# A two-layer streaming encoder step: the head's squares on GpSimd wait for the first weight tile's low part, which is made in halves, and the first feed-forward's down-weight sums get later turns

## The chip, the cores and the metric

One core of one Trainium2 chip. The metric is the device time of the whole kernel in microseconds (us), the median of the timed runs. Before the change it is 2237.28 us, the median of three runs between 2237.07 and 2242.95 us.

## The reference

One inference step of two layers on 1024 prompt frames and 64 sample frames of width 1024. Layer 0 mixes tokens by sliding-window attention with 16 query heads and 4 key heads, layer 1 by a diagonal state-space model. Each mixer and each feed-forward stands between two norms:

```python
for i in range(DEPTH):
    hp = rms_norm(xp, g_pre_mix[i])
    mp = attn_prompt(hp, ...) if i % 2 == 0 else s5_mixer(hp, ...)
    xp = xp + rms_norm(mp, g_post_mix[i])
    hp = rms_norm(xp, g_pre_ffn[i])
    fp = conv_ffn(hp, prev, w_up[i], conv_w[i], conv_b[i], w_down[i])
    xp = xp + rms_norm(fp, g_post_ffn[i])
```

`rms_norm` divides by the root of the mean square over the 1024 channels and multiplies by a gain. `conv_ffn` projects up to 5632 channels, applies a causal convolution of width 3, multiplies the gelu of one half by the other half, and projects down. All is float32.

## The kernel before, in words

The 1088 frames are three blocks of 384, 384 and 320 columns; channels lie on the 128 partitions, eight tiles of them (k = 0 to 7) make the width. A float32 product is made of three matmuls (`mm3`, L224 to L226): with the operand and the weight each split into a high part, rounded to the fast matmul type, and a low part, the rest. L224 multiplies the weight's high part by the operand's low part `hl`, L225 high by high part `hh`, L226 the weight's low part by `hh`. So the third matmul of each k needs the weight's low part.

**Weights** come in units of 128 x 1024 through `raw` (two buffers) by DMAs that SyncE (SP) issues. `split_unit` (L217) makes the high part on ScalarE (ACT) and the low part on VectorE (DVE), both into a tile `whl` of a pool of six. Loads run two units ahead of use (`unit`, `load_ahead`).

**The head** (`build`, from L1532) loads the input and calls `pre_norm` for the three blocks. For each k, ACT makes `hh` (L301) and DVE makes `hl` (L307); for the blocks after the first, GpSimd (POOL) makes three of the eight `hl`, through `gx` (L304, L305). `rstd` sums the squares: for the first block POOL squares two k at a time (L253, four instructions), for the others ACT does (L255); DVE adds (L257, L261). TensorE (PE) then sums over the partitions (L267), DVE finds the root (L272 to L292), PE spreads it over the partitions (L285), and ACT copies it to `rb` (L309). Until the first weight is ready PE runs 14 matmuls on an identity (`fill`, L231). TensorE's first real work is three products of the first block: a key tile (unit 1), and two query tiles (units 2 and 3).

**The first feed-forward** (`ffn` with i = 0) takes 44 up-projection units. Per unit it has 72 matmuls in three blocks; DVE multiplies the results by `rb` into `u` (L415, L417), `conv` (L423 to L425) and `gate` follow, and SP stores the gated tile to `gd` (L442, L443). Beside this, in steps called turns (`aside`, one per unit, 44 in all), run two more jobs:

- *sums*: the down-projection is done with seven products in place of eight, for which sums of the weights (`sums_w`) and of the gated tiles (`sums_g`) are made on DVE. One job is: SP loads `jt` (L356 or L368), in the next turn four additions (L359 to L362, L371 to L377), then SP stores (L363, L378). The dictionary `starts` says in which turn each begins: `sums_w(k)` for k = 0 to 10 in turns 1, 3, ... 21, `sums_g(k)` in turns 24, 26, ... 44.
- *preparation of the state-space layer* (`ssm_prep`), in eight rounds q = 0 to 7: DVE makes `ct` (L1042 to L1047) and `w` (L890 to L895), PE multiplies (`kps`, L1070, and `wps`, L1084), DVE copies to `kt` (L1074, L1075), SP stores it as `kd` and reads it back in another layout with eight DMAs (`tl`, L1105), ACT rearranges (`tp`), and SP stores `prm` from `oc`, `tp` and `b` (L1051, L1107, L1086).

**What sets the order.** Nothing of this is placed by hand on an engine. A scheduler replays the program on a modelled clock and gives each engine, among the instructions that are ready in its model, the one with the smallest priority number; the number counts up as the code emits instructions, and `later(1500)` adds 1500 for the preparation. Each engine, and SP's queue of DMAs, then works strictly in the order found. `order(x, first)` forces an order between two instructions in the schedule; a dependency of class `NoSync` adds no semaphore, one of class `Sync` does.

Of the kernel before, what the change touches and what calls it, by code (L numbers as in the profile page):

```python
# [8 lines left out]
F32 = mybir.dt.float32  # L9
F32R = mybir.dt.float32r  # L10
I32 = mybir.dt.int32
AF = mybir.ActivationFunctionType
# [4 lines left out]
D = 1024  # L17
# [17 lines left out]
KH = KF // 2  # L35
# [8 lines left out]
class Core:  # L44
# [65 lines left out]
    def big(self, shape, name, dt=F32R):  # L110
        return self.wts.tile(shape, dt, name=name, tag="big", bufs=6)

    def order(self, x, first):

        dep = mybir.DependencyInfo(mybir.DependencyClass.NoSync, mybir.DependencyReason.DATA)
        self.tc.add_manual_dep(x.ins, first.ins.name, dep, reason="order")

    @contextmanager
# [13 lines left out]
    sq = {}  # L132
# [77 lines left out]
        return self.split_unit(raw)  # L210

    behind = ()

    def split_unit(self, raw):
        nc = self.nc
        w = self.big([P, 2, D], "whl")
        x = nc.scalar.activation(w[:, 0], raw, AF.Copy), nc.vector.tensor_sub(w[:, 1], raw, w[:, 0].bitcast(F32))  # L217
        for u, v in zip(x, self.behind):
            self.order(u, v)
        return w  # L220
# [17 lines left out]
    def rstd(self, src, n, tag, root, bcast=True, first=False, alt=None, adder=None, fine=False):  # L238
        nc = self.nc
        adder = adder or nc.vector  # L240
        acc = None
        for q in range(4):
            sq = self.n2(n, tag)
            xq = src[:, 2 * q:2 * q + 2]
            if fine and q == 3:

                adder.tensor_add(acc[:, 0], acc[:, 0], acc[:, 1])
                for j in range(2):
                    nc.scalar.activation(sq[:, j], xq[:, j], AF.Square)
                    adder.tensor_add(acc[:, 0], acc[:, 0], sq[:, j])  # L250
                break
            if first:
                nc.gpsimd.tensor_mul(sq, xq, xq)  # L253
            else:
                self.sq[q] = nc.scalar.activation(sq, xq, AF.Square)  # L255
            if q:
                adder.tensor_add(acc, acc, sq)  # L257
            else:
                acc = sq
        else:  # L260
            adder.tensor_add(acc[:, 0], acc[:, 0], acc[:, 1])  # L261
        cuts = [min(c, n - P) for c in range(0, n, P)]
        nt = len(cuts)
        pr = self.sm_ps("pr", int(tag == "sqb") if alt is None else alt)
        st = pr[:, 384:384 + nt]
        for i, c in enumerate(cuts):
            self.last_st = nc.tensor.matmul(st[:, i:i + 1], acc[:, 0, c:c + P], self.ones, start=True, stop=True)  # L267
        v = self.small.tile([P, 4, 4], F32, name="nv" + tag, bufs=3)
        x, hx, r, t = (v[:, i, :nt] for i in range(4))
        if root:  # L270
            nc.scalar.activation(x, st, AF.Sqrt, bias=self.eps)
            nc.vector.tensor_scalar(hx, st, 1e-6, -0.5, op0=ALU.add, op1=ALU.mult)  # L272
            nc.vector.reciprocal(r, x)
            self.refine(r, t, hx)
        else:

            nc.vector.tensor_scalar(x, st, 1e-6, None, op0=ALU.add)
            ri = r.bitcast(I32)
            nc.vector.tensor_scalar(ri, x.bitcast(I32), 1, None, op0=ALU.logical_shift_right)
            nc.vector.tensor_scalar(hx, x, -0.5, None, op0=ALU.mult)  # L280
            nc.vector.tensor_scalar(ri, ri, -1.0, float(MAGIC), op0=ALU.mult, op1=ALU.add)
            for _ in range(3):
                self.refine(r, t, hx)
        for i, c in enumerate(cuts if bcast else []):
            self.last_tr = nc.tensor.transpose(pr[:, c:c + P], r[:, i:i + 1].to_broadcast([P, P]), self.ident)  # L285
        return pr, r
# [54 lines left out]
    def ffn(self, i, h, rb, after, side=None, beside=lambda: None, x=None, g=None):  # L341

        nc, tc, a = self.nc, self.tc, self.a
# [10 lines left out]
        def sums_w(k):  # L354
            x = (jt[:, :2048] if i == 0 else self.yp.tile([P, 2048], F32, name="jw", tag="ypB", bufs=1)).rearrange("p (c h m) -> p c h m", c=2, h=2)
            Q.dma_start(x, a["w_down"][i, k::KH].rearrange("c p (h m) -> p c h m", h=2))  # L356
            yield
            a11, a12, a21, a22 = x[:, 0, 0], x[:, 1, 0], x[:, 0, 1], x[:, 1, 1]
            E.tensor_add(a22, a21, a22)  # L359
            E.tensor_sub(a21, a11, a21)  # L360
            E.tensor_sub(a11, a22, a11)
            E.tensor_sub(a12, a12, a11)  # L362
            Q.dma_start(sd[:, k], x)  # L363

        def sums_g(k):
            x = jt[:, k % 2 * 1536:k % 2 * 1536 + 1536] if i == 0 else ts.tile([P, 1536], F32, name="jg", tag="t2")
            x = x.rearrange("p (c b t) -> p c b t", c=2, b=2)
            Q.dma_start(x, gd[:, k::KH, :768].rearrange("p c (b t) -> p c b t", b=2))  # L368
            yield
            a11, a12, a21, a22 = x[:, 0, 0], x[:, 0, 1], x[:, 1, 0], x[:, 1, 1]  # L370
            v = E.tensor_sub(a11, a12, a11)  # L371
            if i == 1:

                self.order(v, self.last_conv)
            E.tensor_sub(a12, a22, a12)
            E.tensor_sub(a22, a22, a11)
            E.tensor_sub(a21, a21, a22)  # L377
            Q.dma_start(td[:, k], x)  # L378


        w0 = (PLAIN + 1) * i
        starts = {2 * (k + w0) + 1: sums_w(k) for k in range(KH)}
        starts.update({2 * (k + KH) + 2: sums_g(k) for k in range(KH)})
        jobs = {}

# [1223 lines left out]
```

## Time and profile before

| what | us |
|---|---|
| timed runs: median (lowest, highest) | 2237.28 (2237.07, 2242.95) |
| the profiled execution's own time | 2241.03 |
| its span | 2239.2 |
| TensorE busy | 2191.6 (98%) |
| VectorE busy | 1661.3 (74%) |
| ScalarE busy | 1042.3 (47%) |
| GpSimd busy | 412.8 (18%) |

All times in the traces count from the start of the span. TensorE is the busy engine, so time is gained or lost where it stands still: the difference of span and busy time is 47.6 us for the whole kernel. A wait is listed with the engine and line that it was put down to. In the timeline each row has the start, the length, the engine, the line, the operation, what is written and read, and the count; in brackets the idle time before it. Rows of several like instructions are merged. SPq is SP's queue, which issues DMAs; the length is that of the issue, not of the transfer.

### The profile page before, as it was taken

Reading aid. Unit: us, or ns where it says so; the run is one execution under the profiler, and the core shown is the slowest. Engines: PE = TensorE matmul, PEld = TensorE weight load, DVE = VectorE, ACT = ScalarE, POOL = GpSimd, SP = SyncE. Lnnn points to the kernel's source line nnn. Section 1 sums busy time; section 2 is a strip of 40 time slices with the busy share of each in tenths; the row PEclk is TensorE's granted clock in tenths of the full one; section 3 lists DMA queues with packets and bytes.
Section 4 is the critical chain, followed back from the end, with each engine's and each line's share of the span. In section 5 each row is a group of like instructions: output and inputs, shape, how many; then the busy total and the mean of one; then the engine's idle time right before and its main releaser. Section 6 shows DMA issues by size and latency. Waiting matters only on the chain.

```text
span 2239.2 us, 35982 instructions
## 1 busy us (share of the span) xinstructions
PE 2191.6 (98%) x13875; PEld 2117.1 (95%) x13875; DVE 1661.3 (74%) x2886; ACT 1042.3 (47%) x1890; POOL 412.8 (18%) x474
## 2 busy tenths in 40 slices
PE   9999999999999999999988899999999999999997
PEld 8987789999999999999986699999999999999997
DVE  8687647989878877767758855597976776676764
ACT  5255747422343342555545641263555455455543
POOL 5322004200032423000200034352010110110000
PEclk9999999999999999999999899999999999999999
DMA  5100015655355565887749888752266686579772
GB/s 197 37 22 29 20 62 158 241 188 202 122 150 173 176 208 187 274 279 236 233 163 339 263 280 294 249 167 75 87 224 229 218 297 226 196 272 314 218 253 97
DMA packets 208123, 428.47 MB, mean 191 GB/s; under 512 B 23312, under 2 KB 114224, under 8 KB 205008
## 3 DMA queue, kind: packets, MB, share of 16 engines
q1 hardware_dynamic: 175648, 326.56, 44.2%
q0 software_dynamic: 23984, 95.12, 11.9%
q10 hardware_dynamic: 8320, 4.49, 0.8%
q8 instruction: 109, 1.79, 0.3%
q14 instruction: 62, 0.51, 0.1%
HBM read 297.75 MB, written 128.37 MB: 190 GB/s over the span
## 4 chain that ended last, share of the span: by engine, by line
PE 32%; DMA 13%; DVE 9%; issue 4%; ACT 2%; POOL 2%; SPq 0%; DVEq 0%; ACTq 0%; POOLq 0%
PE mm L224 10%; PE mm L226 10%; PE mm L225 10%; DMA sj<-in_w_up 3%; DMA raw<-in_w_down 2%; DMA jw<-in_w_down 2%; DMA raw<-sd 1%; POOL sj L1391 1%; DMA yd<-ys 1%; DVE whl L217 1%; DMA su<-sj 1%; DMA gd<-t 1%; DVE gt L564 1%; DVE t L425 1%; DMA yf<-yd 1%
## 5 line engine op out<-in xcount | busy, mean ns | idle before, releaser
L224 PE MATMUL mm<-hl,whl 128*128 128x384 f32 (+1 forms) x1960 | 643.3, 329 | 4.1 <-DVE hl L307 3.1
L226 PE MATMUL mm<-hh,whl 128*128 128x384 f32 (+1 forms) x1960 | 641.2, 329 | 2.3 <-DVE whl L217 2.3
L225 PE MATMUL mm<-hh,whl 128*128 128x384 f32 (+1 forms) x1960 | 643.1, 328 | 0.0
L224 PEld LDWEIGHTS mm<-hl,whl 128*128 128x128 f32 x1960 | 368.4, 188 | 6.5 <-DVE hl L307 4.7
L226 PEld LDWEIGHTS mm<-hh,whl 128*128 128x128 f32 x1960 | 368.4, 188 | 3.0 <-DVE whl L217 2.9
L225 PEld LDWEIGHTS mm<-hh,whl 128*128 128x128 f32 x1960 | 368.6, 188 | 0.1
L217 DVE TENSOR_TENSOR whl<-raw,whl 128x1024 fp32r<-128x1024 f32 x202 | 254.9, 1263 | 146.7 <-ACT whl L217 146.2
L217 ACT ACTIVATE whl<-raw 128x1024 fp32r<-128x1024 f32 x202 | 213.0, 1058 | 248.1 <-PE mm L226 128.6
L224 PE MATMUL mm<-gt,whl 128*128 128x384 f32 (+1 forms) x968 | 316.8, 327 | 2.9 <-ACT whl L217 2.4
L226 PE MATMUL mm<-gt,whl 128*128 128x384 f32 (+1 forms) x968 | 315.8, 327 | 0.7 <-DVE whl L217 0.7
L225 PE MATMUL mm<-gt,whl 128*128 128x384 f32 (+1 forms) x968 | 315.9, 327 | 0.0
L224 PEld LDWEIGHTS mm<-gt,whl 128*128 128x128 f32 x968 | 181.7, 188 | 3.7 <-ACT whl L217 2.6
L226 PEld LDWEIGHTS mm<-gt,whl 128*128 128x128 f32 x968 | 181.7, 188 | 1.2 <-DVE whl L217 1.2
L225 PEld LDWEIGHTS mm<-gt,whl 128*128 128x128 f32 x968 | 181.8, 188 | 0.0
L195 DVE TENSOR_TENSOR whl<-raw,whl 128x1024 fp32r<-128x1024 f32 x84 | 96.4, 1154 | 72.7 <-ACT whl L194 71.3
L424 DVE SCALAR_TENSOR_TENSOR t<-u,ppt,t 128x1090 f32<-128x1090 f32 x88 | 126.9, 1443 | 5.8 <-ACT t L423 4.1
L194 ACT ACTIVATE whl<-raw 128x1024 fp32r<-128x1024 f32 x84 | 82.6, 987 | 101.8 <-DMA raw<-sd 40.1
L423 ACT ACTIVATE t<-u,ppt 128x1090 f32<-128x1090 f32 x88 | 114.2, 1298 | 26.2 <-DVE u L520 13.6
L425 DVE SCALAR_TENSOR_TENSOR t<-u,ppt,t 128x1090 f32<-128x1090 f32 x88 | 122.0, 1386 | 0.4
L415 DVE TENSOR_TENSOR u<-rb,mm 128x384 f32<-128x384 f32 (+1 forms) x164 | 80.8, 504 | 31.2 <-PE mm L226 26.4
L438 ACT ACTIVATE t<-t 128x1090 f32<-128x1090 f32 x44 | 49.1, 1115 | 113.1 <-DVE t L425 113.1
L564 DVE TENSOR_TENSOR gt<-gr,gt 128x768 fp32r<-128x768 f32 (+2 forms) x106 | 90.5, 881 | 11.1 <-ACT gt L563 10.2
(389 smaller groups left out, 4141.5 us busy)
## 6 DMA issues: line engine op xcount, KB each, us to landing
raw<-in_w_up SPq DMA_DIRECT2D x88, 512.0 KB, 4.4
raw<-in_w_down SPq DMA_DIRECT2D x74, 512.0 KB, 4.4
raw<-sd SPq DMA_DIRECT2D x40, 512.0 KB, 4.9
sj<-in_w_up POOLq DMA_DIRECT2D x68, 256.0 KB, 6.1
su<-sj POOLq DMA_DIRECT2D x34, 512.0 KB, 5.9
raw<-su SPq DMA_DIRECT2D x34, 512.0 KB, 4.6
pm<-prm SPq DMA_DIRECT2D x32, 522.0 KB, 8.2
gr<-td SPq DMA_DIRECT2D x40, 384.0 KB, 5.6
```

Of the source, the lines that this page charges most:

```text
L194: nc.scalar.activation(w[:, 0], raw, AF.Copy)
L195: nc.vector.tensor_sub(w[:, 1], raw, w[:, 0].bitcast(F32))
L217: x = nc.scalar.activation(w[:, 0], raw, AF.Copy), nc.vector.tensor_sub(w[:, 1], raw, w[:, 0].bitcast(F32))
L224: nc.tensor.matmul(out, w[:, 0, sl], xl, start=start, stop=False, skip_group_check=more)
L225: nc.tensor.matmul(out, w[:, 0, sl], xh, start=False, stop=False, skip_group_check=more)
L226: self.last_mm = nc.tensor.matmul(out, w[:, 1, sl], xh, start=False, stop=stop, skip_group_check=more)
L415: nc.vector.tensor_mul(u[:, t0 + 2:t0 + 2 + np_], rb[:, t0:t0 + np_], ps[:, :np_])
L423: nc.scalar.activation(t, u[:, 0:T + 2], AF.Identity, bias=cb(m), scale=cw(0, m))
L424: nc.vector.scalar_tensor_tensor(t, u[:, 1:T + 3], cw(1, m), t, op0=ALU.mult, op1=ALU.add)
L425: self.last_conv = nc.vector.scalar_tensor_tensor(t, u[:, 2:T + 4], cw(2, m), t, op0=ALU.mult, op1=ALU.add)
L438: nc.scalar.activation(ta, ta, AF.Gelu_apprx_tanh)
L564: nc.vector.tensor_sub(x[:, 1, u], raw, x[:, 0, u].bitcast(F32))
```

## The change

Three edits. The first unit's `split_unit` makes its high and its low part in two halves of 512 columns (k 0 to 3, then k 4 to 7). In `rstd` of the first block, POOL's first square gets a true wait (class `Sync`) for the second half of that low part. In the first feed-forward `sums_w(k)` begins in turn min(2k + 5, 12 + k) in place of 2k + 1: turns 5, 7, ... 17, 19, 20, 21, 22.

```diff
-    def order(self, x, first):
+    def order(self, x, first, kind=mybir.DependencyClass.NoSync):
-        dep = mybir.DependencyInfo(mybir.DependencyClass.NoSync, mybir.DependencyReason.DATA)
+        dep = mybir.DependencyInfo(kind, mybir.DependencyReason.DATA)
...
+    first_lo = None
     def split_unit(self, raw):
         nc = self.nc
         w = self.big([P, 2, D], "whl")
+        if self.first_lo is None:
+            for c in (slice(0, 512), slice(512, D)):
+                nc.scalar.activation(w[:, 0, c], raw[:, c], AF.Copy)
+                self.first_lo = nc.vector.tensor_sub(w[:, 1, c], raw[:, c], w[:, 0, c].bitcast(F32))
+            return w
...
             if first:
-                nc.gpsimd.tensor_mul(sq, xq, xq)
+                x = nc.gpsimd.tensor_mul(sq, xq, xq)
+                if q == 0:
+                    self.order(x, self.first_lo, mybir.DependencyClass.Sync)
...
-        starts = {2 * (k + w0) + 1: sums_w(k) for k in range(KH)}
+        starts = {2 * (k + w0) + 1 if i else min(2 * k + 5, 12 + k): sums_w(k) for k in range(KH)}
```

Below, lines of the changed kernel are 7 to 9 higher than the same lines before (L307 is L316, L257 is L266, L217 is L224). What stands on DVE at the very start, from the first low part of the operand on, before:

```order
L307 SCALAR_TENSOR_TENSOR hl<-y,ppt,hh 128x384 x2
L217 TENSOR_TENSOR whl<-raw,whl 128x1024
L307 SCALAR_TENSOR_TENSOR hl<-y,ppt,hh 128x384 x3
L257 TENSOR_TENSOR sqb<-sqb 128x768
L307 SCALAR_TENSOR_TENSOR hl<-y,ppt,hh 128x384 x3
L217 TENSOR_TENSOR whl<-raw,whl 128x1024
L257 TENSOR_TENSOR sqb<-sqb 128x768
```

And on the same engine at the same place in the changed kernel:

```order
L316 SCALAR_TENSOR_TENSOR hl<-y,ppt,hh 128x384 x2
L222 TENSOR_TENSOR whl<-raw,whl 128x512 x2
L316 SCALAR_TENSOR_TENSOR hl<-y,ppt,hh 128x384 x6
L266 TENSOR_TENSOR sqb<-sqb 128x768
L224 TENSOR_TENSOR whl<-raw,whl 128x1024
```

The first addition of squares has moved behind all eight low parts of the first block, and the second addition behind the second unit's low part and the first rows of the next block.

The other place is SP's queue late in the first feed-forward, from the eight reads of round q = 6 of the preparation on. Before (`gd` is the gated tile, `jt` the tile of a sums job, `prm` the prepared parameters):

```order
L1105 DMA tl<-kd 16x8x128 x8
L192 DMA raw<-in_w_down 128x2x512
L442 DMA gd_3999<-t 128x1024
L443 DMA gd_3999<-t 128x64
L1107 DMA prm<-tp 128x4x256
L368 DMA jt<-gd_3999 128x2x768
L1086 DMA prm<-b_6908 128x4x256
L192 DMA raw<-in_w_down 128x2x512
```

The same stretch of SP's queue in the changed kernel:

```order
L1114 DMA tl<-kd 16x8x128 x8
L192 DMA raw<-in_w_down 128x2x512
L1116 DMA prm<-tp 128x4x256
L451 DMA gd_4001<-t 128x1024
L452 DMA gd_4001<-t 128x64
L1095 DMA prm<-b_6899 128x4x256
L377 DMA jt<-gd_4001 128x2x768
L192 DMA raw<-in_w_down 128x2x512
```

The store of the prepared `tp` has moved ahead of the store of the gated tile, and the load of `jt`, which reads `gd` back, behind the store of `b`. The same exchange stands in rounds 2 and 4. On PE the `kps` products of rounds 2 to 6 stand 11 matmuls of the main product further forward, those of rounds 1 and 7 five; those of round 0 stand 11 further back. Up to the last store of a `sums_w` job, SP's queue has the same order in both kernels, so the loads and stores of these jobs have not moved in it.

## The prediction

> **What bounds the kernel now.** I read the page's busy times first, then TensorE's list of waits, then the timeline of the head, and last the stretch of the first feed-forward in which instructions move. The page gives the scale:
>
> ```profile
> span 2239.2 us, 35982 instructions
> PE 2191.6 (98%) x13875; PEld 2117.1 (95%) x13875; DVE 1661.3 (74%) x2886; ACT 1042.3 (47%) x1890; POOL 412.8 (18%) x474
> ```
>
> TensorE stands still for 2239.2 - 2191.6 = 47.6 us in all, so no edit that only removes waits can bring more than that, and a measurement of this kernel can tell about 0.3%, 6.7 us, from no change. TensorE's list of waits shows how little of it lies where the change works (us in total, times, longest):
>
> ```profile
> PE p L1258 <- DMA pm<-prm: 4.6, 5, 2.2
> PE mm L224 <- DVE hl L307: 3.1, 3, 1.6
> PE mm L226 <- DVE whl L217: 3.0, 3, 1.9
> ```
>
> The third row is the head: the longest, 1.9 us, is TensorE waiting for the first weight's low part. The timeline of the head shows why it is late:
>
> ```profile
> 5.36 1.47 POOL L253 TENSOR_TENSOR sqb<-y 128x768 f32<-128x768 f32 x1 [4.29 <-DMA y<-in_x]
> 5.37 1.12 ACT L301 ACTIVATE hh<-y,ppt 128x384 fp32r<-128x384 f32 x2 [3.15 <-DMA y<-in_x]
> 6.02 1.75 DVE L307 SCALAR_TENSOR_TENSOR hl<-y,ppt,hh 128x384 fp32r<-128x384 f32 x2 [4.70 <-ACT hh L301]
> 6.56 1.06 ACT L217 ACTIVATE whl<-raw 128x1024 fp32r<-128x1024 f32 x1
> 7.62 1.47 POOL L253 TENSOR_TENSOR sqb<-y 128x768 f32<-128x768 f32 x1 [0.80 <-DMA y<-in_x]
> 7.69 2.48 DVE L217 TENSOR_TENSOR whl<-raw,whl 128x1024 fp32r<-128x1024 f32 x1
> 10.10 1.66 DVE L307 SCALAR_TENSOR_TENSOR hl<-y,ppt,hh 128x384 fp32r<-128x384 f32 x3
> 10.23 0.69 PE L226 MATMUL mm<-hh,whl 128*128 128x384 f32 x1 [1.94 <-DVE whl L217]
> ...
> 12.55 3.21 DVE L307 SCALAR_TENSOR_TENSOR hl<-y,ppt,hh 128x384 fp32r<-128x384 f32 x3
> 12.71 1.78 POOL L253 TENSOR_TENSOR sqb<-y 128x768 f32<-128x768 f32 x1 [3.62 <-DVE sqb L257]
> 14.47 1.54 POOL L304 TENSOR_SCALAR gx<-y,ppt 128x384 f32<-128x384 f32 x1
> 14.95 0.19 PEld L224 LDWEIGHTS mm<-hl,whl 128*128 128x128 f32 x1 [0.22 <-DVE hl L307]
> 15.68 1.21 DVE L217 TENSOR_TENSOR whl<-raw,whl 128x1024 fp32r<-128x1024 f32 x1
> 15.81 0.19 PEld L224 LDWEIGHTS mm<-hl,whl 128*128 128x128 f32 x1 [0.39 <-DVE hl L307]
> 16.95 0.45 PE L226 MATMUL mm<-hh,whl 128*128 128x384 f32 x1 [0.34 <-DVE whl L217]
> ```
>
> The same subtraction takes 2.48 us beside a square on POOL and 1.21 us without one; three `hl` take 1.66 us alone and 3.21 us beside a square. So a square holds VectorE up by 1.2 to 1.5 us wherever it meets it.
>
> **The head, step by step.** Without the squares `hl` 0 and 1 end at about 7.15 (ACT ends the second `hh` at about 6.5, and one `hl` takes 1.66 / 3 = 0.55). A half of the low part is 1.21 / 2 = 0.6, with its own overhead 0.7; its first high half comes from ACT at about 7.25. So the halves end at about 8.0 and 8.7, and not at 10.17: 1.5 us earlier, and TensorE's third matmul starts at about 8.1 in place of 10.23. So far the two first edits gain.
>
> What is late next is VectorE itself. The first square now starts at 8.7, when VectorE turns to the six `hl` still missing, with the second square behind it. Each holds up one `hl` by 1.2 us. So the second weight's low part, at 15.68 + 1.21 = 16.9 before, now ends at 8.7 + 6 x 0.55 + 0.9 (one addition) + 1.2 + 2 x 1.2 = 16.5; it has only two squares before it, where before the third and one `gx` held VectorE up by 3.21 - 1.66 = 1.55. TensorE's wait at 16.95 is for exactly this part, and it has done the first product by then in both cases. So of 2.1 us at the first matmul 0.4 is left at 16.9. The Trainium skill, "SBUF — State Buffer", section "Who interferes with whom", says that the pair of ports is a lock which the first to issue holds for the whole instruction while the other fully blocks. By that rule each square would cost VectorE its whole 1.47 us, the part would end at 17.0, and the head would bring nothing; by the rows, 1.2 us, it brings 0.4.
>
> Behind that the squares' delay travels on. TensorE's later waits in the head are these, from the timeline:
>
> ```profile
> 39.23 0.83 PE L267 MATMUL pr<-ones,sqb 128*128 128x1 f32 x6 [0.36 <-ACT rb L309]
> 51.98 0.80 PE L267 MATMUL pr<-ones,sqb 128*128 128x1 f32 x6 [0.93 <-DVE sqb L261]
> 63.01 0.54 PE L285 MATMUL pr<-ident,nvsqb 128*128 128x128 f32 x3 [0.89 <-DVE nvsqb L292]
> ```
>
> They wait for VectorE, so TensorE is only ahead at 63 us if VectorE is. VectorE's list of work is later by about 0.8 (the first square ran for 0.66 us while VectorE had nothing to do, 5.36 to 6.02, and now it never does; the split costs 0.1). On the other side the new order leaves one low part (1.21) out ahead of the sum for 51.98, and one rotated key tile out ahead of the root for 63.01, whose rows, and a like one, are
>
> ```profile
> 58.28 2.05 DVE L703 TENSOR_TENSOR kT<-rx 128x384 f32<-128x384 f32 x1
> ...
> 62.87 0.55 DVE L703 TENSOR_TENSOR q<-rx 128x384 f32<-128x384 f32 x1
> ```
>
> (0.55 where no neighbour on POOL holds it up, as the second row). So TensorE is 0.4 us earlier at 52 and between 0.25 later and 0.9 earlier at 63. I take -0.5 for the head, with ends at -1.5 (VectorE is no bound, and all of the first gain stays) and +0.7.
>
> The clock belongs to it. Busy times of the head by stretches of 3.4 us, with the granted clock in the third column from the right:
>
> ```profile
> 6.75:10.17 3.42, 1.07 (x7) 0.56 (x5) 3.42 (x4) 3.42 (x7) 1.55 (x2) 0.96 1.05 405
> 10.17:13.58 3.41, 3.35 (x11) 3.36 (x12) 3.41 (x7) 2.43 (x5) 0.87 (x1) 0.54 1.05 410
> 13.58:17.00 3.42, 3.02 (x16) 2.15 (x14) 3.42 (x4) 2.63 (x5) 2.44 (x2) 1.00 1.05 395
> ```
>
> After a stretch with 1.07 us of work came one at half clock. In the changed kernel the first stretch holds about 2 us of work and the second about 1.7, since TensorE then waits for `hl`. If the second is too little, the half clock falls on 13.58 to 17.0, where TensorE works through the last `hl` at twice the time of each and is up to 0.7 us late for the second weight: this is the +0.7 above. The Trainium skill, "TensorE: Matmul & The Clock Gate", section "Why this matters for your kernels", asks only for gaps above about 3 us to be avoided. By that rule neither kernel loses the clock here and the head stands at -0.5; the trace speaks against it, since a wait of 1.94 us was followed by a half clock.
>
> **The feed-forward.** The loads and stores of `sums_w` keep their order, so this edit does not do what its words say. It acts by the numbers: the preparation gets smaller ones, and part of it moves ahead. TensorE never stands still there: its row of the windows (busy time, instructions) and its groups between 450 and 930 us:
>
> ```profile
> 450.00:930.00 480.00, 480.00 (x2967) 479.72 (x2966) 390.03 (x757) 167.01 (x237) 100.49 (x73) 1.00 0.56 182
> ...
> L226 PE MATMUL mm<-hh,whl 128*128 128x384 f32 (+1 forms) x909 | 301.2, 331 | 0.0
> L1070 PE MATMUL kps<-ct,bd 128*128 128x128 f32 x128 | 23.8, 273 | 0.0
> ```
>
> With no wait to save, this edit can only cost. On VectorE the preparation now goes ahead of low parts and of `u`; that is hidden by the weights, which are loaded two units of 72 matmuls ahead. The tight place is `kps`, which needs the second half of `ct` (L1047). In round 7:
>
> ```profile
> 872.39 0.56 DVE L371 TENSOR_TENSOR jt<-jt 128x384 f32<-128x384 f32 x1 [4.07 <-DMA jt<-gd]
> 878.00 0.75 DVE L1047 SCALAR_TENSOR_TENSOR ct<-m 128x576 f32<-128x576 f32 x1
> 879.05 0.38 PE L1070 MATMUL kps<-ct,bd 128*128 128x128 f32 x2
> ```
>
> `ct` is ready at 878.75 and its first user starts at 879.05: 0.3 us are to spare. A matmul takes 480 / 2967 = 0.16 us. The order puts the product five matmuls forward, 0.8 us, so TensorE waits 0.5 if `ct` stays where it is. `ct` stands behind the wait for `jt`, and SP's queue there has changed:
>
> ```profile
> 859.36 0.41 SPq L442 DMA_DIRECT2D gd<-t  x1
> 862.42 0.48 SPq L1107 DMA_DIRECT2D prm<-tp  x1
> 866.41 0.57 SPq L368 DMA_DIRECT2D jt<-gd  x1
> ...
> 888.67 0.33 SPq L442 DMA_DIRECT2D gd<-t  x1
> 891.35 0.57 SPq L368 DMA_DIRECT2D jt<-gd  x1
> ```
>
> Now `gd` goes out after `prm<-tp`, at about 862.9, and `jt` follows when it has landed: 2.7 us later if it goes as at 888.67, 7.05 if as at 859.36, beside the reads of `tl`, which are now over. That is `jt` at 865.6 to 869.9, from 0.8 earlier to 3.5 later than before. Nearer is the lower end, for the reason just given. I take `jt` unchanged and a wait of 0.5; ends 0 and 2.0.
>
> In the state-space layer, where the head's shift has exchanged a few products, the waits for `pm` are single ones of up to 2.2 us (second fence); I take 0, and 2 us to either side.
>
> **Sum.** -0.5 + 0.5 + 0 = 0 us on the profiled execution's 2241.03, or 2237.3 by the median of the runs, 3.75 lower than that execution.
>
> **The rivals.** *The wait for `ct` runs through the odd rounds (slower).* If `gd` lands in 7 us each time, `jt` comes 3 to 4 us later in rounds 3, 5 and 7, and `kps`, moved forward by up to 11 x 0.16 = 1.8 us, waits: 3.5 to 4.0 in round 7, another 1 to 3 in the two before, and a half clock behind the longest wait, up to 1.7. That is 6.2 to 8.7, say +7.3: 2244.6. It decides from a landing of about 4.5 us on. For it speaks that `prm<-tp`, 512 KB, now goes just ahead; against, that 888.67 shows 2.7 us with small DMAs beside it. *The head loses all its waits (faster).* Without 1.94 + 0.34 + 0.36 + 0.93 + 0.89 = 4.5 us of waits and without the half clock, 1.7, and without the two waits for `hl`, 0.22 + 0.39, it is -6.8: 2230.5. It needs VectorE ahead by as much, and it has lost no work. *The squares take back everything.* Head +0.7, waits for `ct` 2.0: +2.7, 2240.0; this lies within no change.
>
> **How the numbers follow.** Forecast of no change within 0.3%, the third rival in it: 0.87. The slower rival 0.08; the faster one 0.05. Range: -1.5 - 2.0 from the small terms gives 2233.8, and +0.7 + 2.0 + 2.0 gives 2242.0; the runs of before alone reach 5.7 above their median, and with the near part of both rivals I take 2231.5 to 2244.0.
>
> **What would show it.** Right: the first L226 starts near 8.1; one `hl` of the first block takes 1.8 us, twice; the second unit's low part ends at 16.3 to 17; TensorE waits again near 52 and 63; 0 to 2 us of wait before `kps`. Wrong: TensorE well ahead at 63 us; waits above 3 us between 690 and 930; any wait of TensorE in a place named by none of this.

## The result: 0.3% slower, by waits before `kps` in the first feed-forward

The changed kernel takes 2244.33 us, the median of seven runs (2241.99 to 2249.18); the kernel before takes 2237.2 us in the runs beside it. The ratio is 1.003, with a 95% interval of 1.0017 to 1.0042. The forecast was 2237.3 and no change within 0.3%, and its range ended at 2244.0. The median lies 0.3 us above that end, and the ratio put on the forecast's 2237.28 gives 2244.0, so the time stands on the very edge of both. In size and place what came is the slower rival, which had a chance of 0.08; its cause is another, as shown below.

The two profiled executions show only 1 us of it:

```profile
span 2240.2 us, 35976 instructions
PE 2193.1 (98%) x13875; PEld 2117.4 (95%) x13875; DVE 1661.0 (74%) x2887; ACT 1042.8 (47%) x1891; POOL 412.7 (18%) x474
```

This execution is the fastest of its kernel (2241.99, 2.3 below its median), and that of before is 3.8 above its own. So the spans are no measure of the change here, and the place has to be found inside. I do it by one ruler: the main products of TensorE that read `whl`, 11700 in both kernels, are counted from 0, one matmul each, and the start of the same product is compared (the changed kernel minus before).

| product | start before, us | after minus before, us | what lies ahead of it |
|---|---|---|---|
| 2 | 10.2 | -2.24 | first low part, in halves |
| 30 | 17.8 | +0.52 | the `hl` held up by squares, half clock |
| 300 | 64.0 | -0.56 | the head |
| 4000 | 801.2 | -0.22 | feed-forward to round 4 |
| 4368 | 867.5 | +2.65 | rounds 5 and 6 |
| 4500 | 891.6 | +8.35 | round 7 |
| 5200 | 1012.2 | +8.31 | down-projection |
| 6200 | 1306.4 | +2.21 | state-space layer |
| end | 2239.2 | +1.0 | the rest |

**The feed-forward costs 8.5 us**, all of it in rounds 5 to 7; then 6 us of it come back in the state-space layer, in this execution. TensorE's list of waits of the changed kernel (us in total, times, longest) has two rows that before had not, those for `ct` and `kt`:

```profile
PE kps L1079 <- DVE ct L1056: 5.3, 2, 3.8
...
PE mm L231 <- DVE hl L316: 3.6, 5, 1.0
PE p L1267 <- DMA pm<-prm: 2.5, 3, 1.8
...
PE wps L1093 <- DVE kt L1084: 1.0, 1, 1.0
...
PE mm L233 <- DVE whl L224: 0.7, 1, 0.7
```

They are new, 6.3 us, of which 1.5 lie in round 5, 1.0 (for `kt`) in round 6 and 3.85 in round 7. The 1.9 us wait for the first weight's low part is gone. The stretches of the feed-forward, the whole and two around round 7 (TensorE's busy time first, its granted clock third from the right):

```profile
450.00:930.00 480.00, 473.74 (x2919) 472.04 (x2918) 385.01 (x746) 162.36 (x231) 95.76 (x72) 1.00 0.54 179
882.80:886.20 3.40, 1.36 (x6) 1.37 (x7) 3.40 (x8) 2.05 (x4) 0.00 (x0) 0.82 0.05 22
886.20:889.60 3.40, 3.40 (x19) 3.40 (x18) 3.40 (x6) 1.08 (x2) 0.00 (x0) 0.68 0.99 370
```

Before, TensorE was busy for all 480.00; now 6.3 are missing. The clock behind the longest wait adds 0.18 x 3.4 + 0.32 x 3.4 = 1.7. Together that is 8.0 of the 8.5. Round 7 by itself, SP's queue ahead of it, then VectorE, then TensorE:

```profile
841.82 0.37 SPq L1060 DMA_DIRECT2D prm<-oc  x1
842.29 0.57 SPq L377 DMA_DIRECT2D jt<-gd  x1
...
856.24 0.33 SPq L1085 DMA_DIRECT2D kd<-kt  x1
...
869.13 0.38 SPq L1116 DMA_DIRECT2D prm<-tp  x1
869.60 0.46 SPq L451 DMA_DIRECT2D gd<-t  x1
...
873.47 0.57 SPq L377 DMA_DIRECT2D jt<-gd  x1
```

```profile
878.42 0.56 DVE L380 TENSOR_TENSOR jt<-jt 128x384 f32<-128x384 f32 x1 [3.52 <-DMA jt<-gd]
884.03 0.75 DVE L1056 SCALAR_TENSOR_TENSOR ct<-m 128x576 f32<-128x576 f32 x1
```

```profile
880.43 0.38 PE L1079 MATMUL kps<-ct,bd 128*128 128x128 f32 x2
884.84 0.70 PE L1079 MATMUL kps<-ct,bd 128*128 128x128 f32 x2 [3.85 <-DVE ct L1056]
```

The products on the first half of `ct` go at 880.43; those on the second half wait 3.85 for it. `ct` comes 5.6 after the first addition of `jt`, as before (872.39 to 878.00), so it is late because `jt` is. The first addition of `jt` comes 6.03 us later than before (878.42 and 872.39), and TensorE itself is 2.65 later by then, from rounds 5 and 6, so for TensorE `jt` is 3.4 late. With the 0.5 by which the forward move of `kps` uses up its spare time, that gives 3.9; measured are 3.85. The load of `jt` stands at 873.47 in place of 866.41, and the store of `tp`, which it stands behind, at 869.13 in place of 862.42: it is as late as the load.

**The head** went nearly as drawn up, from the timeline of the changed kernel:

```profile
7.24 1.29 DVE L222 TENSOR_TENSOR whl<-raw,whl 128x512 fp32r<-128x512 f32 x2
...
7.98 0.45 PE L233 MATMUL mm<-hh,whl 128*128 128x384 f32 x1
...
8.45 5.68 DVE L316 SCALAR_TENSOR_TENSOR hl<-y,ppt,hh 128x384 fp32r<-128x384 f32 x6
...
10.85 0.45 PE L231 MATMUL mm<-hl,whl 128*128 128x384 f32 x1 [0.95 <-DVE hl L316]
...
12.59 0.69 PE L231 MATMUL mm<-hl,whl 128*128 128x384 f32 x1 [0.65 <-DVE hl L316]
...
14.92 1.21 DVE L224 TENSOR_TENSOR whl<-raw,whl 128x1024 fp32r<-128x1024 f32 x1
15.07 2.38 POOL L260 TENSOR_TENSOR sqb<-y 128x768 f32<-128x768 f32 x1 [2.95 <-DVE sqb L266]
```

Six `hl` take 5.68 where they would take 6 x 0.55 = 3.3: two of them are held up by 1.2 us each. TensorE finds them one by one, and the half clock lasts longer than before:

```profile
6.75:10.17 3.42, 2.38 (x9) 1.43 (x9) 3.36 (x5) 3.42 (x8) 1.56 (x1) 1.00 1.04 399
10.17:13.58 3.41, 2.08 (x6) 1.57 (x7) 3.41 (x5) 2.45 (x5) 1.95 (x2) 0.64 1.05 409
13.58:17.00 3.42, 3.42 (x13) 3.42 (x12) 3.42 (x5) 2.64 (x5) 1.93 (x1) 0.50 1.05 396
17.00:20.40 3.40, 3.40 (x19) 3.40 (x18) 3.40 (x6) 3.40 (x8) 3.38 (x4) 0.86 1.05 391
```

The clock column gives 0.36 x 3.41 + 0.5 x 3.42 + 0.14 x 3.4 = 3.4 us of missing clock; before it was 0.46 x 3.41 = 1.6. Not all of it is lost time, since TensorE also waits for VectorE in these stretches: the run head_alone below, with like waits and a clock of 1.00, is 1.4 us further on at product 30 (-0.90 against +0.52). Later TensorE still waits for VectorE twice, for less than before (0.93 and 0.89); the first wait is now for another row, `rx` (the tile in which keys and queries are rotated), and not for the squares:

```profile
52.62 0.38 PE L734 MATMUL mm<-whl,hl 128*128 128x256 f32 x1 [0.71 <-DVE rx L706]
62.21 0.54 PE L294 MATMUL pr<-ident,nvsqb 128*128 128x128 f32 x3 [0.34 <-DVE nvsqb L301]
```

### The profile page after: what moved, and what is told of

It is laid out like the page before. It is cut to its first block, busy times and chain, and to the rows that moved or that the text cites. A ratio compares the mean times of both kernels' runs of the same rounds, so it can differ in the third digit from the quotient of the medians.

```text
span 2240.2 us, 35976 instructions
## 1 busy us (share of the span) xinstructions
PE 2193.1 (98%) x13875; PEld 2117.4 (95%) x13875; DVE 1661.0 (74%) x2887; ACT 1042.8 (47%) x1891; POOL 412.7 (18%) x474
## 4 chain that ended last, share of the span: by engine, by line
PE 41%; DMA 9%; DVE 6%; issue 2%; ACT 2%; POOL 1%; SPq 0%; ACTq 0%; DVEq 0%; POOLq 0%
PE mm L231 13%; PE mm L233 13%; PE mm L232 13%; DMA sj<-in_w_up 3%; DMA raw<-in_w_down 2%; DMA su<-sj 1%; DVE whl L224 1%; DMA pm<-prm 1%; DVE y L338 1%; DMA yd<-ys 1%; ACT whl L224 1%; POOL sj L1400 1%; DVE y L341 1%; PE p L1333 0%; DVE xs L1147 0%
## 5 line engine op out<-in xcount | busy, mean ns | idle before, releaser
L224 DVE TENSOR_TENSOR whl<-raw,whl 128x1024 fp32r<-128x1024 f32 x201 | 251.7, 1254 | 153.2 <-ACT whl L224 152.8
L224 ACT ACTIVATE whl<-raw 128x1024 fp32r<-128x1024 f32 x201 | 211.9, 1058 | 255.3 <-PE mm L233 139.6
L195 DVE TENSOR_TENSOR whl<-raw,whl 128x1024 fp32r<-128x1024 f32 x84 | 94.5, 1133 | 74.3 <-ACT whl L194 74.0
L433 DVE SCALAR_TENSOR_TENSOR t<-u,ppt,t 128x1090 f32<-128x1090 f32 x88 | 124.3, 1413 | 5.9 <-ACT t L432 4.2
L572 ACT ACTIVATE gt<-gr 128x768 fp32r<-128x768 f32 (+2 forms) x106 | 78.4, 772 | 40.7 <-DMA gr<-gd 25.8
```

What stands on the lines that cost most here:

```text
L433: nc.vector.scalar_tensor_tensor(t, u[:, 1:T + 3], cw(1, m), t, op0=ALU.mult, op1=ALU.add)
L572: nc.scalar.activation(x[:, 0, u], raw, AF.Copy)
```

## The experiments

Twelve kernels ran, four at a time, each group with its own runs of before. The table has the ratio to before with its interval, and from each kernel's one profiled execution the ruler of above at three places (main product 300, 4000 and 5200: at 64, 801 and 1012 us in before); what the feed-forward cost in rounds 5 to 7 is the last column minus the one ahead of it.

| kernel | ratio (95%) | 64 us | 801 us | 1012 us |
|---|---|---|---|---|
| the change | 1.0030 (1.0017 to 1.0042) | -0.56 | -0.22 | +8.31 |
| head_alone | 1.0006 (0.9991 to 1.0021) | -0.55 | -0.47 | -0.47 |
| sums_alone | 1.0039 (1.0027 to 1.0051) | -0.43 | -0.28 | +5.33 |
| tp_on_act | 1.0004 (0.9993 to 1.0014) | -0.07 | -0.47 | -0.52 |
| numbers_back | 1.0019 (1.0006 to 1.0032) | +0.38 | +0.20 | +1.25 |
| queue_only | 0.9992 (0.9980 to 1.0003) | -0.75 | -1.02 | -1.02 |
| halves_only | 1.0009 (0.9999 to 1.0020) | +0.84 | +0.43 | +1.44 |
| wait_only | 1.0009 (0.9995 to 1.0023) | +2.26 | +2.10 | +2.10 |
| behind_hl | 1.0007 (0.9999 to 1.0016) | +2.56 | +3.77 | +3.77 |
| jt_first | 1.0001 (0.9990 to 1.0012) | -0.86 | -1.31 | -0.92 |
| gd_first | 1.0024 (1.0014 to 1.0035) | +0.13 | +0.23 | +5.71 |
| queue_both | 1.0005 (0.9996 to 1.0015) | -0.68 | -0.12 | +0.81 |
| both_undone | 0.9998 (0.9989 to 1.0007) | -0.28 | -0.38 | -0.43 |

### Which part of the change: head_alone and sums_alone

head_alone leaves the turns as they were:

```diff
-        starts = {2 * (k + w0) + 1 if i else min(2 * k + 5, 12 + k): sums_w(k) for k in range(KH)}
+        starts = {2 * (k + w0) + 1: sums_w(k) for k in range(KH)}
```

> The two edits of the head alone, the sums beginning as before. Theory Q (SP's queue: the feed-forward loses the time, because the store of the gated tile now stands behind the store of tp) and theory K (the kps products moved forward are what waits): both expect the head's own -0.5, so 2236.7, between 1.5 faster and 0.7 slower than before, and no wait of TensorE for ct above 0.5 us in the feed-forward. Theory H (the head brings the loss through a later shift): 5 to 7 us slower.

Measured: 1.0006, no wait for `ct`, and -0.47 at 1012 us. sums_alone is the kernel before with the changed `starts` line only:

```diff
-        starts = {2 * (k + w0) + 1: sums_w(k) for k in range(KH)}
+        starts = {2 * (k + w0) + 1 if i else min(2 * k + 5, 12 + k): sums_w(k) for k in range(KH)}
```

> The edit of the sums' turns alone, the head as before. Theories Q and K: 7 to 8 us slower than before (the whole change's 7.1, and 0.5 for the head's part that is missing), with 3.5 to 4 us of wait for ct in round 7. Theory H: within 1 us of before.

Measured: 1.0039, and 5.6 us lost between 801 and 1012 us. TensorE's row:

```profile
PE kps L1079 <- DVE ct L1056: 3.6, 2, 2.1
```

The loss is the feed-forward's, and theory H falls. The place is not quite as expected: round 7 has a wait of 1.4 and not of 3.5 to 4, while the longest, 2.1, stands in round 5 with the half clock behind it. Here the first addition of `jt` in round 7 is 0.9 late for TensorE, and 0.9 + 0.5 is again the wait.

### What in the feed-forward: tp_on_act and numbers_back

```diff
-        nc.sync.dma_start(self.prm[:, 4 * q:4 * q + 4, OKT:OKT + 256], ...)
+        nc.scalar.dma_start(self.prm[:, 4 * q:4 * q + 4, OKT:OKT + 256], ...)
```

> The whole change, but the store of tp is issued by ScalarE, which has made tp, so that SP's queue no longer holds the store of the gated tile behind it; the kps products stay where the change has put them. Theory Q: the gated tile's store in round 7 goes out within 1 us of the tile's last product, jt is 3 to 5 us earlier, the wait for ct in round 7 falls from 3.8 to 1 us or less, and the time is within 1.5 us of before. Theory K: the wait stays above 2 us and the time 5 us or more above before.

Measured: 1.0004, no wait for `ct`, and the gated tile's store of round 6 at 858.04, right at the end of VectorE's product that makes the tile (855.95 + 2.06). TensorE's order is that of the whole change, so kps moved forward costs nothing by itself: theory K falls. But one thing more had moved in this kernel. The schedule came out with the load of `jt` ahead of the store of `oc` in rounds 2, 4 and 6, as before the change; the whole change has `oc` first (841.82 and 842.29 above). So this run could not say which of the two orders it was, and the later runs had to.

```diff
-                with self.later(LOW):
+                with self.later(LOW + 6 * (min(KH, (j + 1) // 2) - sum(min(2 * k + 5, 12 + k) <= j for k in range(KH)))):
```

> The whole change, but the preparation gets back the priority numbers that the later sums took from it (six per job that has not begun yet), so that kps and SP's queue stand as before from round 1 to the middle of round 6, while the sums of the weights still begin later. Theories Q and K both: no wait for ct above 1 us, the time within 1.5 us of before. Theory S (the later sums themselves are dear: their loads and additions collide with other work): still 5 us or more slower than before.

Measured, a miss of both: 1.0019, although the feed-forward costs it 1.05 us. The time is lost behind it, 4.4 us between 1012 and 1306 us. There the order of TensorE, VectorE, ScalarE and SP is that of head_alone, which was 1.0006 and gained 3.8 in the same stretch. What differs there in the two profiled executions is the clock: from 1150 to 1306 us the clock column adds up to 14.0 us of missing clock in numbers_back and 6.7 in head_alone. Its twelve runs fall into two heaps, 2234.13 to 2239.82 (five) and 2244.06 to 2246.98 (seven), and so do those of head_alone (seven up to 2240.91, five from 2243.63). So the sums' later turns are not dear in the feed-forward (theory S falls there; halves_only below has the old order there on every engine and loses 1.0 in the same place), but what sets the heaps stays open.

### Which order in SP's queue: four runs

The change exchanges two pairs in rounds 2, 4 and 6: the store of `tp` goes ahead of the gated tile's store (the one the prediction showed), and the store of `oc` goes ahead of the load of `jt` (which it did not). First, one or both were put into the kernel before by hand. queue_only orders the gated tile's stores behind `tp`:

```diff
+            [self.order(v, self.tp_store[{12: 2, 15: 4, 18: 6}[f]]) for v in x if i == 0 and f in (12, 15, 18)]
```

> The kernel before, with one thing of the change put in by hand: in rounds 2, 4 and 6 the store of tp stands ahead of the gated tile's store in SP's queue, and the stores of b ahead of the load of jt, as in the changed kernel. TensorE's order is that of before, so kps is not moved. Theory Q (the queue alone): the wait for ct that the whole change shows, less what the forward move of kps adds to it (1.8 us in round 5, 0.8 in round 7): none in round 5, about 3 us in round 7, and the time 3 to 4.5 us above before. Theory B (both are needed, since the ScalarE issue took the whole wait away and kps alone cost nothing): no wait above 1 us, and the time within 1.5 us of before.

Measured: 0.9992 and no wait in the feed-forward. The exchange on which the prediction had built its whole doubt costs nothing by itself; theory Q, mine, falls in this form. queue_both adds the other exchange:

```diff
+            ...; [self.order(z, self.oc_store[q]) for q in (2, 4, 6) if i == 0 and k == 3 * q // 2 - 3]
```

> The kernel before, with both exchanges in SP's queue put in by hand in rounds 2, 4 and 6 (tp ahead of the gated tile's store, oc ahead of jt); TensorE's, ScalarE's and GpSimd's order as before, VectorE's but for a few additions of jt. Theory Q2 (SP's queue alone makes the loss): waits for ct of 2 us or more in round 7, time 3 us or more above before. Theory D (the new order of VectorE, with the gated tile's product behind two multiplications of ct, and the earlier kps are needed too): no wait above 1 us, time within 1.5 us of before.

Measured: 1.0005, one wait of 0.6 us, 0.9 us lost. SP's queue alone does not make the loss either. Then each exchange was undone in the changed kernel. jt_first puts `oc` behind `jt` again:

```diff
+            z = Q.dma_start(x, gd[:, k::KH, :768]...); [self.order(self.oc_store[q], z) for q in (2, 4, 6) if i == 0 and k == 3 * q // 2 - 3]
```

> The whole change, with one thing in SP's queue as it was before: in rounds 2, 4 and 6 the load of jt stands ahead of the store of oc again (the change has put oc first). All else, the store of tp ahead of the gated tile's and kps among it, as in the whole change. Theory O (oc ahead of jt makes jt, and with it kt, tl, tp and the next gated tile's store late): no wait for ct above 1 us, time within 1.5 us of before. Theory P (tp ahead of the gated tile's store, together with the new order of the other engines, is what costs): waits for ct of 3 us or more, time 5 us or more above before. Theory C (a chain that needs both exchanges): no wait above 1 us here and in the next run.

Measured: 1.0001, no wait, 0.4 us. gd_first puts `tp` behind the gated tile's store again:

```diff
+            z = Q.dma_start(gd[:, f, SEQ:], ta[:, SEQ + 2:]); [self.order(self.tp_store[q], z) for q in (2, 4, 6) if i == 0 and f == 3 * q // 2 + 9]
```

> The whole change, with the other thing in SP's queue as before: in rounds 2, 4 and 6 the gated tile's store stands ahead of the store of tp, and the load of jt ahead of the store of b; oc stays ahead of jt in the rounds where the change has put it. Theory O: waits for ct of 3 us or more, time 5 us or more above before. Theory P: no wait above 1 us, time within 1.5 us of before. Theory C: as P.

Measured: 1.0024, 5.5 us, with one wait, in round 7, and the half clock behind it:

```profile
PE kps L1079 <- DVE ct L1056: 3.6, 1, 3.6
```

both_undone has both edits.

> The whole change, with both exchanges of rounds 2, 4 and 6 in SP's queue undone, so that on SP only two rows stand otherwise than before in each round (td behind kd or tp); kps and VectorE's order as in the whole change. Theories O, P, C, Q2 and D all: no wait for ct above 1 us, time within 1.5 us of before, since the queue is needed in each. If the wait stays, the loss is in VectorE's order or in kps alone, and the ScalarE issue removed it by something else.

Measured: 0.9998, no wait. So the loss needs `oc` ahead of `jt` (without it, it is gone in jt_first) and the new order on the other engines (without it, it is nearly gone in queue_both); theories O and D fit, and P, Q2 and C fall. Two things weaken this. The edits also moved rows on VectorE: in jt_first the first addition of `jt` stands ahead of the last row of `w` in rounds 2, 4 and 6 and not behind it, and no run moves the one without the other. And in gd_first a row of `conv` (L433) stands behind the first addition of `jt`, so `ct` comes 6.9 us after that addition and not 5.6; of its wait of 3.6, about 1.9 is `jt` being late for TensorE, 1.3 that row and 0.5 the forward move of `kps`.

How the exchange becomes a delay of 4 us shows in round 4. SP's transfers of `jt` there (KB, us from issue to landing), before, in the changed kernel and in jt_first:

```profile
jt<-gd SPq DMA_DIRECT2D x1, 768.0 KB, 4.7
```

```profile
jt<-gd SPq DMA_DIRECT2D x1, 768.0 KB, 6.9
```

```profile
jt<-gd SPq DMA_DIRECT2D x1, 768.0 KB, 5.7
```

With the 512 KB of `oc` ahead the landing takes 1.2 us or more longer. The issue is later too, since the gated tile that it reads is late from the rounds ahead. The changed kernel, then jt_first:

```profile
760.43 0.37 SPq L1060 DMA_DIRECT2D prm<-oc  x1
760.90 0.57 SPq L377 DMA_DIRECT2D jt<-gd  x1
```

```profile
757.29 0.57 SPq L377 DMA_DIRECT2D jt<-gd  x1
757.96 0.55 SPq L1060 DMA_DIRECT2D prm<-oc  x1
```

The two loads are issued 3.6 apart, of which 1.1 is TensorE's own distance (-0.22 and -1.31 at 801 us). Then VectorE, with GpSimd beside it. The changed kernel:

```profile
765.64 0.68 DVE L904 TENSOR_TENSOR w<-m 128x512 f32<-128x512 f32 x1
767.79 1.34 DVE L380 TENSOR_TENSOR jt<-jt 128x384 f32<-128x384 f32 x1 [1.47 <-DMA jt<-gd]
769.05 2.53 DVE L434 SCALAR_TENSOR_TENSOR t<-u,ppt,t 128x1090 f32<-128x1090 f32 x1
771.51 1.53 DVE L384 TENSOR_TENSOR jt<-jt 128x384 f32<-128x384 f32 x1
...
774.41 0.22 DVE L1083 SCALAR_TENSOR_TENSOR kt<-dv,kps 128x16 f32<-128x16 f32 x1
...
766.41 1.18 POOL L899 TENSOR_TENSOR m<-tq,tp 128x576 f32<-128x576 f32 x1 [22.11 <-DVE w L904]
```

And jt_first:

```profile
763.04 0.56 DVE L380 TENSOR_TENSOR jt<-jt 128x384 f32<-128x384 f32 x1 [0.80 <-DMA jt<-gd]
763.52 0.69 DVE L904 TENSOR_TENSOR w<-m 128x512 f32<-128x512 f32 x1
764.12 1.35 DVE L434 SCALAR_TENSOR_TENSOR t<-u,ppt,t 128x1090 f32<-128x1090 f32 x1
765.38 1.54 DVE L384 TENSOR_TENSOR jt<-jt 128x384 f32<-128x384 f32 x1
...
768.30 0.22 DVE L1083 SCALAR_TENSOR_TENSOR kt<-dv,kps 128x16 f32<-128x16 f32 x1
...
764.29 2.22 POOL L899 TENSOR_TENSOR m<-tq,tp 128x576 f32<-128x576 f32 x1 [23.17 <-DVE w L904]
```

GpSimd starts its six operations of 128 x 576 as soon as `w` is done. In the changed kernel VectorE then stands waiting for `jt` and comes back while they run: 1.34 and 2.53 in place of 0.56 and 1.35. In jt_first it waits for `jt` ahead of `w`; its row of 1.35 then starts 0.17 ahead of GpSimd's first operation, and it is that one which takes longer, 2.22 in place of 1.18. From GpSimd's start to `kt` it is 8.0 us in the changed kernel and 4.0 in jt_first. Behind `kt` hang its store, the eight reads of `tl`, `tp`, and the store of `tp`; and the load of the next `jt` stands behind that store in each of these kernels (only tp_on_act has it on another queue). In gd_first the store of `tp` is at 867.60 and the load at 868.06, although the gated tile went out at 861.65; but the tile landed only at 868.02, 6.4 us later, so either of the two alone would have held the load. In jt_first the store of `tp` is at 859.5, and it does no harm that the gated tile waits for it.

### What the head is worth: halves_only, wait_only, behind_hl

All three have the sums as before. halves_only drops the squares' wait:

```diff
-                if q == 0:
-                    self.order(x, self.first_lo, mybir.DependencyClass.Sync)
```

> Of the head only the first low part in halves; the squares begin as before, the sums too. The first half still meets a square, so the third matmul starts at 8.6 to 9.3 (before 10.23, whole change 8.0). Theory V (VectorE and GpSimd's hold on it set the end of the head, whatever TensorE gains early): main products at 64 us within 0.6 us of before. Theory T (what TensorE gains at the first wait stays): they are about 1 us ahead. The time of the whole kernel is within 2 us of before by both.

Measured: third matmul at 9.32, and +0.84 at 64 us, just outside theory V's 0.6 and on the other side of theory T. wait_only has the low part in one piece:

```diff
-            for c in (slice(0, 512), slice(512, D)):
+            for c in (slice(0, D),):
```

> Of the head only the squares' wait, for the undivided low part, and the sums as before. The low part takes 1.2 us in place of 2.48 and the third matmul starts at 8.9 to 9.1; then two or three low parts of the operand are held up as in the whole change. Theory V: main products at 64 us within 0.6 us of before. Theory T: about 1.2 us ahead. The time of the whole kernel is within 2 us of before by both.

Measured: third matmul at 8.15, 2.1 ahead of before and better than expected, and 2.26 behind at 64 us. behind_hl waits for the last low part of the first block:

```diff
-                    self.order(x, self.first_lo, mybir.DependencyClass.Sync)
+                    self.order(x, self.last_hl, mybir.DependencyClass.Sync)
```

> The two edits of the head, but the squares wait for the last of the first block's eight low parts in place of the first weight's; the sums as before. TensorE finds its low parts 0.55 us apart, doesn't lose the clock, and is 2 to 3 us ahead at 18 us. Theory V: the squares then hold VectorE up in the next block and in the root, and of the lead 0.8 us or less is left at 64 us. Theory T: 2 us or more of it are left there, and the kernel is about 2 us faster than before.

Measured: 3.75 us ahead at 31 us, clock 1.00 in all stretches to 40 us, and 2.56 behind at 64 us. The whole lead and more went here:

```profile
PE mm L734 <- DVE rx L706: 4.6, 1, 4.6
```

```profile
40.00:65.00 25.00, 20.38 (x143) 20.04 (x142) 22.41 (x43) 7.58 (x12) 9.57 (x12) 0.86 0.26 85
```

TensorE waits 4.6 us for VectorE, until 53.5, and the granted clock of the stretch is 0.86. Theory T falls in all three. V's direction holds, but not its bound: the later products are not within 0.6 but up to 2.6 late, so something costs more than the squares' delay alone; that it is how VectorE's rows fall out is read from where the waits lie, and not shown.

No version was faster than the kernel before by more than can be measured: the lowest ratios, 0.9992 and 0.9998, have intervals that reach over 1.

## Where the prediction held and where it failed, by its steps

**Right.** The halves end at 8.53 (forecast 8.7), the third matmul starts at 7.98 (8.1), two `hl` are held up by 1.2 us each, the second unit's low part ends at 16.13 (16.3 to 17, so a little ahead), TensorE waits near 52 and 62, and the head stands at -0.56 (-0.5) at 64 us. The `hl` beside a square take 1.82 in place of 0.61, and they end at 10.80, 12.54 and 17.87, each 0.41 or 0.42 behind the end of a square (10.38, 12.12, 17.46). The Trainium skill, "SBUF — State Buffer", "Who interferes with whom", says that the first to issue has the shared ports for its whole instruction and the other fully blocks; the trace agrees. The prediction set the two against each other, and wrongly: it took the rule to cost VectorE the whole length of a square, but the first `hl` comes to its turn 0.37 us behind the start of its square (8.98 and 8.61), so what is left to wait is less than the square's 1.77.

**Right only by its size: the head's -0.5.** The seven profiled executions with both head edits stand at 64 us at -0.86 to +0.38, mean -0.26; the four with the old head at -0.75 to 0, mean -0.47. The spread covers it, and no gain is shown. The step "of 2.1 us at the first matmul 0.4 is left at 16.9" didn't come: the changed kernel was 0.52 behind at 17.8, because the half clock lasted 3.4 us of missing clock in place of 1.6, where I had moved it and not lengthened it. In head_alone, with the same waits, the clock stayed at 1.00 and TensorE was 0.90 ahead there; at 64 us both stand alike. The Trainium skill, "TensorE: Matmul & The Clock Gate", Part 1, says that the window of 3.4 us by which the clock is granted runs free of the kernel; like waits with and without a half clock agree with that, but do not prove it.

**Wrong: "I take `jt` unchanged and a wait of 0.5; ends 0 and 2.0".** The 0.5 was right: it is the part of round 7's wait that does not come from `jt`. What failed is `jt` "unchanged": it was 3.4 late for TensorE, and the waits were 5.3 us for `ct` and 1.0 for `kt`, with 1.7 of half clock behind the longest. These are nearly the slower rival's terms (3.85 in round 7 against its 3.5 to 4.0, 1.7 against up to 1.7), but by luck: its condition was that the gated tile takes 4.5 us or more to land, and the tile of round 6 landed in 3.9 in the changed kernel, and in 6.2 in jt_first, which has no wait. The error begins one step earlier, in "Now `gd` goes out after `prm<-tp`, at about 862.9". That left the store of `tp` where it was, at 862.42, and asked only how fast the gated tile would land behind it. The store was at 869.13. I had looked at the exchange just ahead of `jt`'s load, and taken the times of all that stands ahead of it from the old trace. But its cause lies rounds back, with the store of `oc` ahead of the load of `jt`, which stands in SP's new order of rounds 2, 4 and 6 and which the prediction does not name, and it works through VectorE and GpSimd. queue_only shows that the exchange named costs nothing in the old order; jt_first shows that the loss goes when the other is undone, together with the one row on VectorE that moves with it.

**Right: the edit does not do what its words say.** numbers_back has the later sums and 1.05 us of loss in the feed-forward; the cost was in the preparation's new order.

**Too narrow: "In the state-space layer ... I take 0, and 2 us to either side".** From 1012 to 1306 us the profiled executions differ from that of before by -6.1 (the change) to +4.4 us (numbers_back), and one kernel differs from run to run: the 34 runs of before beside the last group go from 2233.86 to 2242.69. TensorE waits there for `pm` and VectorE again and again, and its clock in 1250 to 1300 us is 0.91 in one execution and 1.00 in others. That this is where the runs' spread arises is argued from one execution of each kernel, not shown. In the two profiled executions +8.5 in the feed-forward and -6.1 here nearly cancel in the span; that is luck, and no merit of the sum.

## What to carry to other kernels

When a schedule moves a transfer ahead of another, follow what stands behind it for a whole round of the loop and don't take the neighbours' old times: here the row next to the wait was harmless by itself, and the one that cost stood a round and more earlier, on another buffer. A small change of priority numbers is tested by putting single rows back, one by one and both, in the changed kernel, and also by putting them into the old one: the first says what is needed, the second what is enough. Look also at which other rows the scheduler moves with each edit, since they belong to what was tested. And a lead of TensorE at the start of a stage whose end waits for VectorE is worth nothing (3.75 us of lead became 2.56 us of lag).

## What the runs showed of the hardware

- The half clock is not a fixed price of a wait: with like waits in the head 3.4 us of granted clock were missing in one execution and nothing in head_alone, and TensorE was 1.4 us further back for it.
- A load of 768 KB issued 0.5 us behind a store of 512 KB on the same queue took 6.9 us to land in rounds 4 and 6, against 4.7 and 5.4 (before) or 5.7 and 5.8 (jt_first) with that store behind it.
- Of a VectorE row and a GpSimd operation that meet, the later one is stretched. Rows of VectorE that come while GpSimd works go from 0.56 to 1.34 (128 x 384) and from 1.35 to 2.53 us (128 x 1090), and the `hl` of the head end 0.41 or 0.42 us behind the square that they met; where VectorE's row started 0.17 us ahead, GpSimd's operation went from 1.18 to 2.22. So when VectorE is kept waiting just as GpSimd starts, it pays for the wait and then for the slower rows.
